# A decoder layer's up projections with seven block products for eight in half of the k groups, weight sums made by adding DMAs and VectorE, and the hidden columns in three parts

## The chip, the cores and the metric

The kernel runs on one core of a Trainium2 chip, as one launch. The metric is the device time of a launch in microseconds; the median of three runs of the kernel before is 2240.55 us.

## The reference, cut to what matters

One decoder layer on 256 tokens of 2048 features: a SwiGLU network, a token-mixing block, and a second SwiGLU network, each followed by a LayerNorm over the sum with its input. All is float32. The change lies in the two SwiGLU networks:

```
def swiglu(x, w_up, w_down):                    # x [256, 2048], D_FF = 5632
    a, u = jnp.split(x @ w_up, 2, axis=-1)      # w_up [2048, 2 * 5632]
    return (jax.nn.silu(a) * u) @ w_down        # w_down [5632, 2048]

h = layer_norm(ALPHA * h + 0.5 * swiglu(h, w_ffn1_up, w_ffn1_down), ln1_g, ln1_b)
...
h = layer_norm(ALPHA * h + 0.5 * swiglu(h, w_ffn2_up, w_ffn2_down), ln3_g, ln3_b)
```

## The kernel before, in words

**Split products.** Every large matrix product is made from float32r parts. A float32 page is split into h, its rounded value, and l, the rest, so that h + l is the page exactly (`split`, L90 to L93): ScalarE (ACT) writes h (L92), then VectorE (DVE) writes l = page - h (L93). A product of two split matrices takes three matmuls on TensorE (PE): ah with wh, ah with wl, al with wh (L133). One matmul has 128 rows of k, 128 tokens (stationary) and 512 weight columns (moving), and adds into a PSUM bank of 128 x 512.

**A gemm** (L121) makes 512 output columns for both token tiles (tt = 0, 1). It goes over groups of 512 rows of k. For each group the weights, 1 MB, come in one DMA on the queue of SyncE (SP) into one of three `raw` buffers (L104 to L106), are split as two halves of 128 x 1024 into `wh` and `wl` (four buffers of each), and each half feeds 2 kt x 2 tt x 3 = 12 matmuls. A half can be split only when one of the four `wh` and `wl` pairs is free again, that is, when PE is through with the half four before it.

**A SwiGLU network** (`ffn`, L188). The hidden width has 11 columns of 512 (j). A column takes two gemms of four groups, a with the weights up[j] and u with up[11 + j]: 2 x 4 x 24 = 192 matmuls. Then ACT makes tanh of a (L206), DVE makes silu(a) * u from the two accumulators (L207, L208), and `place` turns the result back to features by 8 transposes on PE (L166) and a split into two pages (L92, L93); `later` and `tick` put that behind the first group of the next column's products. After all 11 columns the down product runs: four gemms of 11 groups (`project_norm`, L215), whose accumulators DVE adds to the residual (L235).

**Order of the work.** A scheduler orders the instructions on each engine when the program is built, and every engine then runs its own list strictly in that order, waiting on semaphores. DMAs are issued on three queues: SP (weights), ACT (the input x transposed, `in_xT`, L185) and POOL (GpSimd's software queue: residuals L223, scales L228, rows of results L267). `project_norm` issues the residuals' loads after the last column.

**The start.** x is loaded from `in_xT` page by page on ACT's queue (L185) beside the first weights, each page split before the products of its group.

Of the kernel before, what the change touches and what calls it, by code (L numbers as in the profile page):

```python
# [9 lines left out]
F32 = mybir.dt.float32  # L10
# [26 lines left out]
GL0 = 10  # L37


class Layer:  # L40
# [32 lines left out]
    def page(self, dt=F32, tag="pg"):  # L73
        return self.tile(tag, [P, 1024], dt, 27 if tag == "pg" else 6)
# [4 lines left out]
    def tmp(self, shape=(P, 512), dt=F32):  # L79
        return self.tile("tmp", list(shape), dt, 4)  # L80

    def acc(self):
        self.n += 1
        return self.ps.tile([P, 512], F32, name=f"acc_{self.n}", tag="acc", bufs=4)

    def tr(self):
        self.n += 1
        return self.ps.tile([P, 512], F32, name=f"tr_{self.n}", tag="tr", bufs=4)
# [10 lines left out]
    def raw(self, shape=(P, 4, 512)):  # L99
        return self.tile("raw", list(shape), F32, 3)  # L100

    def load_w(self, src, paged=False, cut=None):
        """[128, 4, 512] of weights -> two halves of (h, l); cut(i) goes with half i."""
        raw = self.raw()  # L104
        if cut is None:
            self.nc.sync.dma_start(raw, src)  # L106
        out = []
        for i in range(2):
            if cut is not None:
                cut(i)  # L110
                self.nc.sync.dma_start(raw[:, 2 * i:2 * i + 2, :], src[:, 2 * i:2 * i + 2, :])
            if paged:
                h, l = (self.page(F32R).rearrange("p (k n) -> p k n", k=2) for _ in range(2))
            else:
                h = self.tile("wh", [P, 2, 512], F32R, 4)
                l = self.tile("wl", [P, 2, 512], F32R, 4)
            self.split(h, l, raw[:, 2 * i:2 * i + 2, :])
            out.append((h, l))
# [35 lines left out]

    def act_pages(self, hp, lp):
        """Pages of four k tiles by 256 tokens -> act() of gemm."""
# [5 lines left out]
    def transpose4(self, src):  # L162
        """[128, 512] -> four [128, 128] transposes side by side in PSUM."""
# [9 lines left out]
    def to_feature(self, src, hpage, lpage, tt, scale=None):  # L173
        """[128 tokens, 512] in SBUF -> h and l of the four k tiles in the pages."""
# [7 lines left out]
    def load_split_T(self, src, hp, lp, i, c=slice(0, 1024), paged=False):  # L182
        """Columns c of page i of src [128, 16, 256]."""
# [4 lines left out]
    def ffn(self, xh, xl, w_up, w_down, resid, g, b, finish, before_last=None, before=None, cut=None,  # L188
# [3 lines left out]
        hh, hl = [], []  # L192

        def place(ts, ph, pl):
            for tt in range(2):
                self.to_feature(ts[tt], ph, pl, tt)
            yield

        for j in range(NFF):
            a = self.gemm(act, w_up[j], 4, head=4 if j == 0 and before is None else 0, before=before if j == 0 else None,  # L200
                          cut=cut if j == 0 else None)
            u = self.gemm(act, w_up[NFF + j], 4)
            ph, pl = self.page(F32R), self.page(F32R)
            ts = [self.tmp(), self.tmp()]
            for tt, t in enumerate(ts):
                nc.scalar.activation(t, a[tt], AF.Tanh, scale=0.5)  # L206
                nc.vector.scalar_tensor_tensor(t, t, 1.0, a[tt], op0=ALU.add, op1=ALU.mult)  # L207
                nc.vector.scalar_tensor_tensor(t, t, 0.25, u[tt], op0=ALU.mult, op1=ALU.mult)  # L208
            self.later(place(ts, ph, pl))
            hh.append(ph)  # L210
            hl.append(pl)
        self.project_norm(self.act_pages(hh, hl), w_down, KF // 4, resid, g, b, finish, before_last,
                          4 if before_last is None else 2, filler)

    def project_norm(self, act, w, groups, resid, g, b, finish, before_last=None, tail=4, filler=None):  # L215
        """finish(LN(ALPHA * resid + act @ w))."""
        nc = self.nc
        z = [self.page(tag="gt") for _ in range(ND)]
        gb = [self.page(tag="gt" if i < 2 else "pg") for i in range(ND)]
        stats = [self.tile("stats", [P, ND, 6], F32, 2) for _ in range(2)]  # L220
        for n in range(ND):
            for tt in range(2):
                self.mark = nc.gpsimd.dma_start(z[n][:, 512 * tt:512 * tt + 512],  # L223
                                                resid[tt * P:(tt + 1) * P, 512 * n:512 * n + 512])
        with self.after_mark():
            for n in range(ND):
                for i, v in enumerate((g, b)):
                    nc.gpsimd.dma_start(gb[n][:, 512 * i:512 * i + 512],  # L228
# [461 lines left out]
```

## Time and profile before

| | |
|---|---|
| three runs | 2240.1, 2240.55, 2241.12 us; median 2240.55 |
| the profiled execution | span 2238.4 us from its first to its last instruction; no other time of its own is given, so what lies around the span is taken from the median: 2.15 us |
| PE busy | 2215.9 us, 99% of the span, 10056 matmuls |
| DVE busy | 1248.9 us, 56% |
| ACT busy | 958.2 us, 43% |
| DMA | 442 MB at a mean of 198 GB/s |

The share of busy time says who works, not who is waited for; the chain that ended last says that: 96% of it is PE. A busy PE is not PE at its fastest, since matmuls are pipelined (one shows some 390 ns while the next starts after some 227); the pace is read from stretches of the chain.

### The profile page before, as it was taken

Reading aid. Unit: us, or ns where it says so; the run is one execution under the profiler, and the core shown is the slowest. Engines: PE = TensorE matmul, PEld = TensorE weight load, DVE = VectorE, ACT = ScalarE, POOL = GpSimd, SP = SyncE. Lnnn points to the kernel's source line nnn. Section 1 sums busy time; section 2 is a strip of 40 time slices with the busy share of each in tenths; the row PEclk is TensorE's granted clock in tenths of the full one; section 3 lists DMA queues with packets and bytes.
Section 4 is the critical chain, followed back from the end, with each engine's and each line's share of the span. In section 5 each row is a group of like instructions: output and inputs, shape, how many; then the busy total and the mean of one; then the engine's idle time right before and its main releaser. Section 6 shows DMA issues by size and latency. Waiting matters only on the chain.

```text
span 2238.4 us, 24924 instructions
## 1 busy us (share of the span) xinstructions
PE 2215.9 (99%) x10056; PEld 1838.5 (82%) x10056; DVE 1248.9 (56%) x1404; ACT 958.2 (43%) x1075; POOL 51.2 (2%) x93
## 2 busy tenths in 40 slices
PE   8999999999999999999999999999999999999997
PEld 6888888888888888888888888878888888888886
DVE  5555555554455757675566556675555555454445
ACT  4444444443334444554444444444444444443332
POOL 0000000010000100000000000010000000000000
PEclk9999999999999999999999999999999999999999
DMA  7555555565556645455655556666555555565553
GB/s 261 191 188 188 188 188 188 189 253 205 199 188 228 233 170 182 169 184 188 207 179 194 199 193 220 235 221 239 188 188 188 189 190 191 188 211 197 188 192 128
DMA packets 65956, 442.34 MB, mean 198 GB/s; under 512 B 7905, under 2 KB 7905, under 8 KB 15537
## 3 DMA queue, kind: packets, MB, share of 16 engines
q1 hardware_dynamic: 57888, 414.21, 52.4%
q0 software_dynamic: 6656, 22.36, 3.4%
q10 hardware_dynamic: 1296, 4.19, 0.5%
q8 instruction: 78, 1.28, 0.2%
q14 instruction: 38, 0.30, 0.0%
HBM read 434.44 MB, written 6.29 MB: 197 GB/s over the span
## 4 chain that ended last, share of the span: by engine, by line
PE 96%; DVE 2%; DMA 1%; issue 0%; ACT 0%; POOL 0%; POOLq 0%; ACTq 0%; DVEq 0%
PE acc L133 93%; PE tr L166 2%; PE tr L282 1%; DMA pg<-in_xT 1%; DVE wl L93 0%; DVE pg L562 0%; DMA tmp<-in_w_pool 0%; DVE gt L252 0%; DVE m L561 0%; PE tr L314 0%; DVE pg L93 0%; DVE gt L254 0%; DVE stats L236 0%; DVE gt L235 0%; POOL mv L245 0%
## 5 line engine op out<-in xcount | busy, mean ns | idle before, releaser
L133 PE MATMUL acc<-wh,pg 128*128 128x512 f32 x5120 | 1594.2, 390 | 0.0
L93 DVE TENSOR_TENSOR wl<-raw,wh 128x1024 fp32r<-128x1024 f32 x772 | 944.4, 1224 | 917.2 <-ACT wh L92 916.7
L92 ACT CAST wh<-raw 128x1024 fp32r<-128x1024 f32 x772 | 812.7, 1054 | 1130.6 <-PE acc L133 1099.2
L133 PEld LDWEIGHTS acc<-wh,pg 128*128 128x128 f32 x5120 | 961.2, 188 | 198.3
L133 PE MATMUL acc<-wl,pg 128*128 128x512 f32 x2560 | 996.4, 389 | 0.0
L133 PEld LDWEIGHTS acc<-wl,pg 128*128 128x128 f32 x2560 | 480.7, 188 | 98.0
L133 PE MATMUL acc<-wh,gt 128*128 128x512 f32 x1056 | 332.8, 391 | 7.8 <-ACT wh L92 7.2
L133 PEld LDWEIGHTS acc<-wh,gt 128*128 128x128 f32 x1056 | 198.9, 189 | 49.3 <-ACT wh L92 7.2
L133 PE MATMUL acc<-wl,gt 128*128 128x512 f32 x528 | 206.4, 391 | 1.0 <-DVE wl L93 1.0
L133 PEld LDWEIGHTS acc<-wl,gt 128*128 128x128 f32 x528 | 99.6, 189 | 22.2 <-DVE wl L93 1.8
L92 ACT CAST pg<-tr 128x512 fp32r<-128x512 f32 x82 | 44.7, 586 | 20.4 <-PE tr L166 19.8
L93 DVE TENSOR_TENSOR pg<-tr,pg 128x512 fp32r<-128x512 f32 x82 | 52.5, 682 | 0.6 <-ACT pg L92 0.3
L206 ACT ACTIVATE tmp<-acc 128x512 f32<-128x512 f32 x44 | 26.2, 595 | 26.0 <-PE acc L133 26.0
L207 DVE SCALAR_TENSOR_TENSOR tmp<-tmp,acc 128x512 f32<-128x512 f32 x44 | 30.1, 684 | 10.3 <-ACT tmp L206 10.3
L133 PE MATMUL acc<-pg,pg 128*128 128x512 f32 x144 | 34.5, 392 | 0.8 <-DVE pg L93 0.7
L133 PEld LDWEIGHTS acc<-pg,pg 128*128 128x128 f32 x144 | 26.8, 188 | 7.1 <-DVE pg L93 1.6
L166 PEld LDWEIGHTS tr<-ident,tmp 128*128 128x128 f32 x240 | 27.9, 140 | 3.9
L166 PE MATMUL tr<-ident,tmp 128*128 128x128 f32 x240 | 31.0, 272 | 0.0
L208 DVE SCALAR_TENSOR_TENSOR tmp<-tmp,acc 128x512 f32<-128x512 f32 x44 | 28.1, 680 | 0.0
L235 DVE SCALAR_TENSOR_TENSOR gt<-gt,acc 128x512 f32<-128x512 f32 x24 | 15.7, 682 | 21.5 <-PE acc L133 21.5
L282 PE MATMUL tr<-pg,pg 128*128 128x256 f32 (+2 forms) x168 | 26.3, 302 | 0.0
L93 DVE TENSOR_TENSOR pg<-raw,pg 128x1024 fp32r<-128x1024 f32 x18 | 21.7, 1217 | 4.5 <-ACT pg L92 4.5
(99 smaller groups left out, 418.4 us busy)
## 6 DMA issues: line engine op xcount, KB each, us to landing
raw<-in_up SPq DMA_DIRECT2D x175, 1024.0 KB, 4.8
raw<-in_down SPq DMA_DIRECT2D x88, 1024.0 KB, 4.8
raw<-in_w_in SPq DMA_DIRECT2D x88, 1024.0 KB, 4.8
raw<-in_w_out SPq DMA_DIRECT2D x16, 1024.0 KB, 5.1
raw<-in_w_kv SPq DMA_DIRECT2D x8, 1024.0 KB, 5.0
raw<-in_br_att SPq DMA_DIRECT2D x8, 1024.0 KB, 4.8
h_d<-gt POOLq DMA_DIRECT2D x16, 256.0 KB, 3.6
raw<-in_br_pool SPq DMA_DIRECT2D x4, 1024.0 KB, 4.8
```

Of the source, the lines that this page charges most:

```text
L92: self.nc.scalar.copy(h, src)
L93: self.nc.vector.tensor_sub(l, src, h.bitcast(F32))
L133: nc.tensor.matmul(accs[tt], lhsT=a, rhs=b, start=kt == 0 and i == 0, stop=kt == kts - 1 and i == 2)
L166: self.nc.tensor.transpose(t[:, i * P:(i + 1) * P], src[:, i * P:(i + 1) * P], self.ident)
L206: nc.scalar.activation(t, a[tt], AF.Tanh, scale=0.5)
L207: nc.vector.scalar_tensor_tensor(t, t, 1.0, a[tt], op0=ALU.add, op1=ALU.mult)
L208: nc.vector.scalar_tensor_tensor(t, t, 0.25, u[tt], op0=ALU.mult, op1=ALU.mult)
L235: nc.vector.scalar_tensor_tensor(zz, zz, ALPHA, accs[tt], op0=ALU.mult, op1=ALU.add)
L282: self.nc.tensor.matmul(out, lhsT=a, rhs=b, start=start and i == 0, stop=stop and i == 2)
```

## The change

**Seven products for eight.** For each column but the first of a network, a and u are made together by `seven`. In a group of 512 rows of k the operands are seen as 2 x 2 blocks: tokens 0 to 127 and 128 to 255, k in two halves of 256, and the two weight matrices w0 = up[j], w1 = up[11 + j]. In groups 0 and 1 seven block products, in Winograd's form of Strassen's scheme, replace eight; groups 2 and 3 keep eight products, with one of the token operands replaced by a difference so that they can share the banks. A column so takes 2 x 7 x 6 + 2 x 48 = 180 matmuls for 192, in seven PSUM banks. Ten columns in each of the two networks are made so: 20 columns.

**Sums of tokens** are made once per network (`forms`) on DVE, beside the first column.

**Sums of weights.** In a seven group three halves are loaded and split as they are: b00, b10 (w0) and b11 (w1). Then b00 becomes b00 + b01 by a DMA on POOL's queue that adds from HBM (L230), is split (t1), becomes t1's sum plus b11 by DVE (L239), is split (t2), becomes that plus b10 by DVE (L243), and is split (t4); b11 becomes b11 + b01 by a second adding DMA (L241), which needs L239 to have read b11, and is split (t3). So a seven group has seven splits for four, two DVE sums and two adding DMAs of 512 KB.

**Combination.** Behind a column ACT copies bank 1 and DVE makes seven sums and differences of the banks (L283 to L289) before the SwiGLU arithmetic (now L351, L352).

**Columns in three parts.** `HIDDEN` cuts the 11 columns into 4, 4 and 3. After each part the down product runs over that part's groups alone, and its four results are added to the residual's pages (`Norm.add`). The residuals' loads (`Norm.load`) are called after the first part, the scales' before the last down product.

**Buffers.** `raw` is nine buffers of half the size (a weight group comes as two DMAs of 512 KB), pages are 23 and 6 for 27 and 6, tmp six for four, and the accumulators and transposes share all eight PSUM banks. x takes ordinary pages, not those of tag gt. Loads of the memory input stand at the first two groups of the last down gemm.

```diff
+PAGES = dict(pg=23, gt=6)
+HIDDEN = ((0, 4), (4, 8), (8, NFF))
+SEVEN = (True, True, False, False)
...
-        return self.ps.tile([P, 512], F32, name=f"acc_{self.n}", tag="acc", bufs=4)
+        return self.ps.tile([P, 512], F32, name=f"acc_{self.n}", tag="ps", bufs=8)
...
-    def raw(self, shape=(P, 4, 512)):
-        return self.tile("raw", list(shape), F32, 3)
+    def raw(self, shape=(P, 2, 512)):
+        return self.tile("raw", list(shape), F32, 9)
...
+    def forms(self, hp, lp, modes):
...
+            a = self.page()
+            nc.vector.tensor_add(a, hp[g].bitcast(F32), lp[g].bitcast(F32))
+            if seven:
+                q = a.rearrange("p (j k i t) -> p i j k t", j=2, k=2, i=2)
+                f = self.page()
+                fv = f.rearrange("p (f k t) -> p f k t", f=4, k=2)
+                nc.vector.tensor_sub(fv[:, 0], q[:, 1, 0], q[:, 1, 1])
+                nc.vector.tensor_sub(fv[:, 1], fv[:, 0], q[:, 0, 0])
+                nc.vector.tensor_sub(fv[:, 2], q[:, 0, 0], q[:, 1, 0])
+                nc.vector.tensor_add(fv[:, 3], q[:, 0, 1], fv[:, 1])
+                h, l = self.page(F32R), self.page(F32R)
+                self.split(h, l, f)
...
+        def singles(g, end):
+            b00, b10 = self.load_half(w0[g], 0), self.load_half(w0[g], 1)
+            b11 = self.load_half(w1[g], 1)
+            s00 = self.halves(b00)
+            nc.gpsimd.dma_start(b00, w1[g][:, 0:2, :], accum_op=ALU.add)
+            product(g, 1, quarter(g, 0, 0), s00, g == sevens[-1])
+            s10 = self.halves(b10)
+            product(g, 2, quarter(g, 0, 1), s10, end)
+            s11 = self.halves(b11)
+            product(g, 3, form(g, 3), s11, end)
+
+            def sums():
+                t1 = self.halves(b00)
+                nc.vector.tensor_add(b00, b00, b11)
+                product(g, 5, form(g, 0), t1, end)
+                nc.gpsimd.dma_start(b11, w1[g][:, 0:2, :], accum_op=ALU.add)
+                t2 = self.halves(b00)
+                nc.vector.tensor_add(b00, b00, b10)
+                product(g, 6, form(g, 1), t2, g == sevens[-1])
+                t3 = self.halves(b11)
+                product(g, 7, form(g, 2), t3, g == sevens[-1])
+                t4 = self.halves(b00)
+                product(g, 4, quarter(g, 1, 1), t4, end)
+
+            return sums
...
+        behind = None
+        for g in range(groups):
+            end = g == groups - 1
+            if modes[g]:
+                after = singles(g, end)
+            else:
+                eight(g, end)
+                after = None
+            if behind is not None:
+                behind()
+            behind = after
+            self.tick()
...
+        u, c00, v, c11 = (self.tmp() for _ in range(4))
+        nc.scalar.copy(u, banks[1])
+        nc.vector.tensor_add(c00, u, banks[2])
+        nc.vector.tensor_add(u, u, banks[6])
+        nc.vector.tensor_add(v, u, banks[7])
+        nc.vector.tensor_sub(u, banks[5], u)
+        nc.vector.tensor_sub(c11, banks[5], v)
+        nc.vector.tensor_add(u, u, banks[3])
+        nc.vector.tensor_add(v, v, banks[4])
+        return [[c00, u], [v, c11]]
...
+        for lo, hi in HIDDEN:
+            hh, hl = [], []
+            for j in range(lo, hi):
+                if j == 0:
+                    a = self.gemm(act, w_up[0], 4, head=4 if before is None else 0, before=before, cut=cut)
+                    forms = self.forms(xh, xl, SEVEN)
+                    u = self.gemm(act, w_up[NFF], 4)
+                else:
+                    c = self.seven(act, forms, SEVEN, w_up[j], w_up[NFF + j])
+                    a, u = ([c[tt][i] for tt in range(2)] for i in range(2))
...
+            if lo == 0:
+                norm.load()
+            if last:
+                norm.load_scales()
+            w = [w_down[n][lo:hi] for n in range(ND)]
+            norm.add(self.act_pages(hh, hl), w, hi - lo, lo == 0, last, before_last,
+                     3 if before_last is None else 2)
```

**How it moves instructions.** The first place is DVE's list where one column ends and the next begins. Before (wl is a half's l, L208 the last step of the SwiGLU arithmetic, pg<-tr the turned result):

```order
L93 TENSOR_TENSOR wl_991<-raw_988,wh_990 128x1024
L93 TENSOR_TENSOR wl_995<-raw_988,wh_994 128x1024
L93 TENSOR_TENSOR wl_1039<-raw_1036,wh_1038 128x1024
L208 SCALAR_TENSOR_TENSOR tmp_978<-tmp_978,acc_838 128x512
L208 SCALAR_TENSOR_TENSOR tmp_979<-tmp_979,acc_839 128x512
L93 TENSOR_TENSOR wl_1043<-raw_1036,wh_1042 128x1024
L93 TENSOR_TENSOR wl_1073<-raw_1070,wh_1072 128x1024
L93 TENSOR_TENSOR wl_1077<-raw_1070,wh_1076 128x1024
```

In the change the same place on DVE reads as follows; L286 is the first combination that needs the column's last product, and wl_1185, wl_1196 belong to group 1 of the next column, whose group 0 has been split before these rows:

```order
L286 TENSOR_TENSOR tmp_1109<-acc_873,tmp_1109 128x512
L287 TENSOR_TENSOR tmp_1112<-acc_873,tmp_1111 128x512
L288 TENSOR_TENSOR tmp_1109<-tmp_1109,acc_817 128x512
L289 TENSOR_TENSOR tmp_1111<-tmp_1111,acc_908 128x512
L351 SCALAR_TENSOR_TENSOR tmp_1123<-tmp_1123,tmp_1110 128x512
L96 TENSOR_TENSOR wl_1185<-raw_1178,wh_1184 128x1024
L352 SCALAR_TENSOR_TENSOR tmp_1123<-tmp_1123,tmp_1109 128x512
L351 SCALAR_TENSOR_TENSOR tmp_1124<-tmp_1124,tmp_1111 128x512
L96 TENSOR_TENSOR wl_1196<-raw_1180,wh_1195 128x1024
L352 SCALAR_TENSOR_TENSOR tmp_1124<-tmp_1124,tmp_1112 128x512
```

Eight combining steps and two splits stand there where two steps stood. The rows that follow directly on DVE, with the third split of group 1 and the sums of group 0 (raw_1131 is its b00, raw_1133 its b10, raw_1135 its b11):

```order
L96 TENSOR_TENSOR pg_1122<-tr_1171,pg_1121 128x4x128
L96 TENSOR_TENSOR wl_1206<-raw_1182,wh_1205 128x1024
L96 TENSOR_TENSOR wl_1216<-raw_1131,wh_1215 128x1024
L239 TENSOR_TENSOR raw_1131<-raw_1131,raw_1135 128x1024
L96 TENSOR_TENSOR wl_1229<-raw_1131,wh_1228 128x1024
L243 TENSOR_TENSOR raw_1131<-raw_1131,raw_1133 128x1024
L96 TENSOR_TENSOR wl_1241<-raw_1135,wh_1240 128x1024
L96 TENSOR_TENSOR wl_1252<-raw_1131,wh_1251 128x1024
```

They are t1, the first sum, t2, the second sum, t3 and t4 in that order, all behind the combining of the column before.

The second place is ACT's list at the program's start, with the loads of x (in_xT) that ACT issues. Before:

```order
L185 DMA pg_82<-in_xT 128x512
L185 DMA pg_91<-in_xT 128x512
L185 DMA pg_124<-in_xT 128x1024
L92 ACT_TABLE_LOAD
L92 CAST gt_71<-pg_82 128x512
L92 CAST wh_87<-raw_81 128x1024
```

In the change:

```order
L322 DMA pg_81<-in_xT 128x512
L95 ACT_TABLE_LOAD
L95 CAST pg_71<-pg_81 128x512
L95 CAST wh_87<-raw_85 128x1024
L322 DMA pg_91<-in_xT 128x512
L95 CAST wh_97<-raw_95 128x1024
L322 DMA pg_125<-in_xT 128x1024
L95 CAST pg_71<-pg_91 128x512
L95 CAST wh_131<-raw_129 128x1024
L95 CAST wh_137<-raw_135 128x1024
L95 CAST pg_72<-pg_125 128x1024
L95 CAST wh_171<-raw_169 128x1024
```

The second and third loads have moved behind casts of weights; the fourth, pg_165, follows wh_171, and the fifth, pg_205, follows the cast of the fourth.

The third place is POOL's queue at the start. Before, its first loads of x's rows (L223) follow the last up column. In the change they stand right behind the constants:

```order
L540 DMA pscale_67<-in_pool_scale 128x4
L476 DMA gt_1478<-in_x 128x512 x2
L476 DMA gt_1479<-in_x 128x512 x2
L476 DMA gt_1480<-in_x 128x512 x2
L476 DMA gt_1481<-in_x 128x512 x2
L485 DMA gt_5103<-in_g 128x512
L485 DMA gt_5103<-in_b 128x512
L485 DMA gt_5104<-in_g 128x512
L485 DMA gt_5104<-in_b 128x512
L230 DMA raw_437<-in_up 128x1024
```

Twelve loads of 256 KB, 3 MB, are so issued at the start, ahead of the first adding DMA.

## Rows read from the trace of the kernel before

**Rows 1.** The page, part 1: busy time, share and instructions of each engine.
```profile
PE 2215.9 (99%) x10056; PEld 1838.5 (82%) x10056; DVE 1248.9 (56%) x1404; ACT 958.2 (43%) x1075; POOL 51.2 (2%) x93
```
**Rows 2.** Waits, whole span: who waited for whom, us in total, times, longest.
```profile
ACT wh L92 <- PE acc L133: 1099.2, 680, 5.7
DVE wl L93 <- ACT wh L92: 916.7, 699, 3.2
...
PE acc L133 <- ACT wh L92: 7.2, 1, 7.2
```
**Rows 3.** Chain of work, 100 to 200 us: start, us, what.
```profile
105.88 43.54 PE acc L133 x192
149.42 0.88 PE tr L166 x8
150.29 43.54 PE acc L133 x192
```
**Rows 4.** Busy time in windows: one column; the down product. Columns: PE, PEld, DVE, ACT, POOL, clock, DMA, GB/s.
```profile
105.88:150.29 44.41, 44.41 (x201) 36.86 (x201) 23.28 (x22) 18.93 (x21) 0.00 (x0) 1.00 0.52 189
...
505.60:761.30 255.70, 255.70 (x1130) 211.67 (x1130) 140.54 (x142) 103.80 (x101) 8.00 (x11) 1.00 0.59 207
```
**Rows 5.** Groups by line: busy us, mean ns | idle before, releaser.
```profile
L93 DVE TENSOR_TENSOR wl<-raw,wh 128x1024 fp32r<-128x1024 f32 x772 | 944.4, 1224 | 917.2 <-ACT wh L92 916.7
L92 ACT CAST wh<-raw 128x1024 fp32r<-128x1024 f32 x772 | 812.7, 1054 | 1130.6 <-PE acc L133 1099.2 <-issue 7.5 <-ACT gt L549 6.6
```
**Rows 6.** Timeline of DVE, two dense stretches: start, us, engine, line, what.
```profile
758.42 1.41 DVE L254 SCALAR_TENSOR_TENSOR gt<-gt,mv,pg 128x512 f32<-128x512 f32 x2
759.75 2.35 DVE L93 TENSOR_TENSOR wl<-raw,wh 128x1024 fp32r<-128x1024 f32 x2
...
764.53 4.27 DVE L93 TENSOR_TENSOR pg<-tr,pg 128x512 fp32r<-128x512 f32 x7
...
1493.32 1.22 DVE L93 TENSOR_TENSOR pg<-raw,pg 128x1024 fp32r<-128x1024 f32 x1
1494.45 1.22 DVE L93 TENSOR_TENSOR wl<-raw,wh 128x1024 fp32r<-128x1024 f32 x1
```
**Rows 7.** DMA issues of POOL's queue in four windows: KB each, us to landing.
```profile
tmp<-in_b_gate POOLq DMA_DIRECT2D x1, 256.0 KB, 4.7
pg<-in_consts POOLq DMA_DIRECT2D x1, 512.0 KB, 5.5
raw<-in_band POOLq DMA_DIRECT2D x1, 1024.0 KB, 6.2
pg<-in_consts POOLq DMA_DIRECT2D x1, 512.0 KB, 9.4
```
**Rows 8.** Chain of work at the start: start, us, what.
```profile
1.66 10.94 DMA pg<-in_xT
...
12.64 7.64 DMA pg<-in_xT
...
22.67 37.92 PE acc L133 x166
```
**Rows 9.** Busy time in one window at the start; columns as in rows 4.
```profile
10.00:15.00 5.00, 5.00 (x18) 3.95 (x17) 2.72 (x4) 2.81 (x4) 0.00 (x0) 1.00 0.98 363
```
**Rows 10.** Timeline of PE at the start.
```profile
7.24 1.22 PE L133 MATMUL acc<-wh,gt 128*128 128x512 f32 x2 [7.24 <-ACT wh L92]
...
10.09 0.63 PE L133 MATMUL acc<-wh,gt 128*128 128x512 f32 x1
10.52 0.63 PE L133 MATMUL acc<-wl,gt 128*128 128x512 f32 x1
...
13.50 0.40 PE L133 MATMUL acc<-wl,gt 128*128 128x512 f32 x1
13.74 0.62 PE L133 MATMUL acc<-wh,gt 128*128 128x512 f32 x2
```

More of the change, by code (lines that the diff above doesn't have):

```diff
@@ L73, in page @@
     def page(self, dt=F32, tag="pg"):
-        return self.tile(tag, [P, 1024], dt, 27 if tag == "pg" else 6)
+        return self.tile(tag, [P, 1024], dt, PAGES[tag])
     def pages(self, n, dt=F32R, tags=()):
@@ L110, in load_w @@
                 cut(i)
[L111 to L118, printed above, removed]
+            out.append(self.halves(self.load_half(src, i), paged))
         return out
@@ L153, in gemm @@
         return accs
+    def forms(self, hp, lp, modes):
+        nc = self.nc
+        out = []
+        for g, seven in enumerate(modes):
+            a = self.page()
[11 more added lines that the diff above has]
+            else:
+                q = a.rearrange("p (k i t) -> p i k t", k=4, i=2)
+                f = self.tmp()
+                nc.vector.tensor_sub(f.rearrange("p (k t) -> p k t", k=4), q[:, 0], q[:, 1])
+                both = self.page(F32R)
+                h, l = both[:, :512], both[:, 512:]
+                self.split(h, l, f)
+            out.append((h, l))
+        return out
@@ new lines, in seven, with product, quarter, form @@
+    def seven(self, act, forms, modes, w0, w1):
+        nc = self.nc
+        banks = {}
+        groups = len(modes)
+        sevens = [g for g in range(groups) if modes[g]]
+        first = set()
+        def product(g, bank, lhs, w, last):
+            if bank not in banks:
+                banks[bank] = self.acc()
+            for k in range(2):
+                ah, al = lhs(k)
+                for i, (a, b) in enumerate(((ah, w[0]), (ah, w[1]), (al, w[0]))):
+                    nc.tensor.matmul(banks[bank], lhsT=a, rhs=b[:, k, :], start=bank not in first,
+                                     stop=last and k == 1 and i == 2)
+                    first.add(bank)
+        def quarter(g, i, j):
+            return lambda k: act(4 * g + 2 * j + k, i)
+        def form(g, i):
+            return lambda k: tuple(v[:, (2 * i + k) * P:(2 * i + k + 1) * P] for v in forms[g])
+        def singles(g, end):
[21 more added lines that the diff above has]
+            return sums
+        def eight(g, end):
+            b00, b10 = self.load_half(w0[g], 0), self.load_half(w0[g], 1)
+            b01, b11 = self.load_half(w1[g], 0), self.load_half(w1[g], 1)
+            s00 = self.halves(b00)
+            product(g, 2, quarter(g, 0, 0), s00, False)
+            product(g, 4, quarter(g, 1, 0), s00, False)
+            s10 = self.halves(b10)
+            product(g, 2, quarter(g, 0, 1), s10, end)
+            product(g, 4, quarter(g, 1, 1), s10, end)
+            s01 = self.halves(b01)
+            product(g, 3, form(g, 0), s01, False)
+            product(g, 5, quarter(g, 1, 0), s01, False)
+            s11 = self.halves(b11)
+            product(g, 3, form(g, 1), s11, end)
+            product(g, 5, quarter(g, 1, 1), s11, end)
+        behind = None
[3 more added lines that the diff above has]
+                after = singles(g, end)
+            else:
+                eight(g, end)
[4 more added lines that the diff above has]
+            self.tick()
+        assert behind is None
+        u, c00, v, c11 = (self.tmp() for _ in range(4))
[8 more added lines that the diff above has]
+        return [[c00, u], [v, c11]]
@@ L191, in ffn @@
         act = self.act_pages(xh, xl)
-        hh, hl = [], []
+        norm = Norm(self, resid, g, b)
+        forms = None
         def place(ts, ph, pl):
@@ L196, in place @@
                 self.to_feature(ts[tt], ph, pl, tt)
[L197 to L211, printed above, removed]
@@ L258, in norm_to_feature, with project_norm @@
+        norm.finish(finish, filler)
+    def project_norm(self, act, w, groups, resid, g, b, finish):
+        norm = Norm(self, resid, g, b)
+        norm.load()
+        norm.load_scales()
+        norm.add(act, w, groups, True, True, None, 4)
+        norm.finish(finish)
     def norm_to_feature(self, dram):
@@ L361, in layer_kernel @@
     h2_d = L.dram.tile([SEQ, D_MODEL], F32, name="h2_d")
-    xh = L.pages(ND, tags=("gt",) * 3)
-    xl = L.pages(ND, tags=("gt",) * 3)
+    xh = L.pages(ND)
+    xl = L.pages(ND)
     mem = ([], [])
     def load_mem(g):
-        if g in (4, 6, 8, 10):
+        for _ in range(2 if g < 2 else 0):
             for p in mem:
```

144 lines of the change are left out of this document (89 added, 55 removed).

## The prediction

> **What bounds the kernel now.** I read the page's busy times first: PE is busy for 99% of the span, DVE for 56%, ACT for 43% [rows 1]. Busy does not say bound, so the waits came next. ACT's casts wait for PE 1099.2 us in all, DVE's splits wait for ACT 916.7 us, and PE waits for either of them once, 7.2 us at the start [rows 2]: the weights' chain DMA, ACT, DVE always runs ahead until its four buffers are full. Third, the chain of work over two up columns: 192 matmuls in 43.54 us, then 8 transposes in 0.88, and again [rows 3]. So a column lasts 44.4 us, and a matmul 43.54 / 192 = 0.2268 us. In a column DVE works 23.3 us and ACT 18.9 [rows 4]. PE alone sets the time here, and only fewer matmuls or a new wait can change it.
>
> The median of the runs is 2240.55 us, the profiled span 2238.4. I make the sum on the span's pieces and add it to the median; the 2.15 us around the span stay.
>
> **What the change removes.** 12 matmuls in each of 20 columns: 12 x 0.2268 = 2.72 us a column, 54.4 us in all. PE's own work in a column becomes 180 x 0.2268 + 0.88 = 41.7 us.
>
> **What it adds on DVE.** Dense stretches give the pace: a 128 x 1024 step follows the last after 1.13 us, though one lasts 1.22; seven 512-wide steps with PSUM take 4.27, so 0.60 each; two 512-wide steps with both inputs in SBUF take 1.33 to the next start, 0.665 each [rows 6]. A column needs 22 splits and 4 sums (26 x 1.13 = 29.4), 7 combinations and 2 turned results (9 x 0.60 = 5.4) and 4 SwiGLU steps (2.7): 37.5 us. ACT needs 22 casts of 1.05 [rows 5] and some small ones, 26 us. Both are under 41.7, so by sums alone nothing is lost. But the order on DVE decides, and I follow one column with a column before it.
>
> **The path through a column.** Zero is the end of the last product before.
> - DVE has by then split the three single halves of the new group 0 (its four buffers allow no more), which keep PE for 18 x 0.2268 = 4.1 us. The rest of DVE's list stands behind L286, which needs that last product: four combinations (4 x 0.60 = 2.4), four SwiGLU steps (2.66), a turned result (0.6), three splits of group 1 and t1 (4 x 1.13 = 4.5), then the first sum, which has to wait until t1 is through and be through itself (1.3). It ends at 11.5 us.
> - Only then can POOL issue the second adding DMA; ACT's cast of t3 waits for it, and the casts of t4 and of group 2 stand behind that on ACT. From before I know plain loads on this queue: 256 KB land after 4.7 us, 512 KB after 5.5 and, beside much traffic, 9.4, 1 MB after 6.2 [rows 7]. An adding DMA of 512 KB reads 512 KB in HBM and 512 KB in SBUF, so I take the row of 1 MB, **6.2 us**, with 4.7 and 9.4 as the ends. It lands at 17.7.
> - Cast of t3 1.05, its split 1.22, split of t4 1.13, then five matmuls of t4's product and three transposes (1.46): PE starts group 2 at 22.6 us. Without waits it would have started at 4.1 + 4.1 + 5.4 + 0.9 = 14.5.
> - Group 2 and the sums of group 1: t1 of group 1 gets a buffer when the first half of group 2 is done (2.72); cast 1.05, split 1.22, sum 1.25, DMA 6.2, cast 1.05, splits 1.22 and 1.13, five matmuls 1.13: 17.0 us. PE's own work for this stretch is 72 x 0.2268 = 16.3, so this wait is nearly hidden.
> - Group 3: 48 x 0.2268 = 10.9.
>
> The sum is 22.6 + 17.0 + 10.9 = **50.5 us against 44.4, 6.1 more**. 14 of the 20 columns are so. The two behind a network's first column lack the combinations: 47.1, 2.7 more each. The four that follow a down product have neither: the first sum is through at 4.1 + 1.05 + 1.22 + 1.22 = 7.6, and the column takes 46.2, 1.8 more each. Together 14 x 6.1 + 2 x 2.7 + 4 x 1.8 = **98 us**. The first adding DMA (L230) needs no place in the sum: it is issued some 5 us before zero, and t1's turn on ACT comes past 4.
>
> With 4.7 us for the DMA the three kinds take 48.3, 44.9 and 44.0, in all 54 us more; with 9.4 every column is 6.4 longer than in the sum, in all 226 more. Even a DMA that cost nothing would leave 11.5 + a cast, t2, the second sum, t3 and t4 = 17.4, so 46.1 for a full column.
>
> The Trainium skill, DMA: Bandwidth & Descriptors (Anatomy of one DMA, SWDGE path), puts a DMA of this queue at about 2.0 us and its bytes at 436 GB/s, an estimate of 3.2 us for 512 KB, by which the sum would be some 25 us. The rows speak against it: 256 KB, 2.6 by that rule, took 4.7.
>
> **The start.** x's pages load on ACT's queue. Before, three loads went out at once, and the page that ended last landed after 10.94 + 7.64 us; PE runs without a stop from 22.67 [rows 8], while the DMA engines are busy all the time (0.98) [rows 9]. Now loads two to five stand behind casts on ACT, each cast waiting for weights or a buffer, and 3 MB of residuals and scales are issued on POOL's queue at the same time. Two loads of some 7.6 us are so put behind each other, of which the products of three k groups hide about half: I take **8 us**, between 2 (loads of 4.7 us) and 12.
>
> **At no cost.** The token sums (`forms`), at most 18 DVE steps or 14 us per network, lie beside a first column in which DVE idles some 21 us [rows 4]; without that cover they would cost 28 us in all. The 32 further additions of down results take 19 us of DVE beside down products, where DVE works 140.5 us of 255.7 [rows 4]. Five loads of half a megabyte for four per seven group are 20 MB more, where the DMA engines are busy for half the time (0.52) [rows 4]; their own waits are in the path above. The middle of the layer keeps its products; shared PSUM banks and smaller buffers may move it by 5 us either way.
>
> The sum: 2240.55 + 98 + 8 = **2347 us**.
>
> **Rivals.**
> - *The chain is hidden.* If DVE's 37.5 us and the DMAs stayed beside PE's 41.7, the saving would come through: 2240.55 - 54.4 + 8 = 2194. For it speak the busy sums, and the 1.5 us of idle time before each split now. Against it: L286 stands ahead of group 1's splits and t1. It decides at a column path of 44.4 us, and the path has 46.1 with a free DMA, so it needs DVE's steps to be a fifth shorter than their rows.
> - *The adding DMA lands in about 3 us.* Then the full column takes 46.9 and the total is 2274. No row of that queue is so short. This is also what the page's rule above gives.
> - *PE's clock falls in the gaps.* Between t2's and t3's products PE would idle some 3.7 us. At the start, after 7.24 us without work, matmuls come 0.43 us apart (10.09 to 10.52), as at 1.2 GHz, and later 0.24 (13.50 to 13.74) [rows 10]; the granted clock printed there is 1.00 [rows 9], so I go by the spacing. Some 11 matmuls ran so, 0.2 us longer each: 2.3 us a gap, 46 us in 20 columns, in all 2393. Against it: the gap is half as long. The Trainium skill, TensorE: Matmul & The Clock Gate (Part 1), says that the throttled state is the default and that activity lifts it; the start agrees, no row shows a gap of this length later.
> - *The adding DMA is slow*, 9.4 us: 2347 + 128 = 2475. For it speaks that no row shows an adding DMA.
>
> **How the numbers follow.** The forecast (DMA of 5 to 7.5 us, 2305 to 2400) has 0.56, the fallen clock 0.18, the slow DMA 0.13, the fast one 0.06, the hidden chain 0.07. The range runs from 2290, the 4.7 us end with a start of 2 us and some slack, to 2480, the slow DMA; it leaves out the two quick cases. No change, within 0.2% (which is what a measurement of this kernel can tell), lies in none of the cases but between them: 0.01. Faster is the hidden chain, 0.07; slower 0.92.
>
> **What would show it.** Right: a column of 50 us, PE waiting in it once for the cast or split of t3 for several us; L241 issues that land after 6 us; DVE busy for three quarters of the up stretch; the down products at 0.227 us a matmul as before; PE's continuous run starting some 8 us later. Wrong: columns under 44 us, no PE wait behind t3, or waits of PE that end on a PSUM bank instead; matmuls 0.43 us apart behind the gaps mean the third rival.

## The result and the profile after

The changed kernel takes **2428.88 us** (median of 4 runs, 2427.76 to 2433.55) against 2240.84 us for the kernel before beside it: ratio 1.0844, 95% interval 1.0831 to 1.0856. It is slower, as forecast, and inside the range, but by 188 us where the sum said 106. It lies outside the narrower band, 2305 to 2400 us, that the forecast gives for a DMA of 5 to 7.5 us. The profiled span is 2427.9 us, 189.5 longer than before's.

The page, part 1, and the waits of PE, which before waited once, 7.2 us [rows 1, 2]; columns of a wait: in total, times, longest.

```profile
PE 2258.0 (93%) x9816; PEld 1822.4 (75%) x9816; DVE 1600.8 (66%) x1812; ACT 1086.2 (45%) x1223; POOL 120.2 (5%) x174
```
```profile
PE acc L215 <- ACT wh L95: 91.3, 65, 3.9
PE acc L215 <- DVE wl L96: 40.9, 54, 0.9
PE tr L303 <- DVE gt L524: 9.9, 2, 9.5
```

PE does 240 matmuls fewer, and is busy 42 us longer: some of them run at half speed. Its waits are now in the new products (L215), 119 of them in 20 columns. Three columns in windows (before [rows 4]: 44.41 us, PE without a gap, DVE 23.28, ACT 18.93, clock 1.00, DMA 0.52), the first and last of these full ones, the middle one behind a down product:

```profile
114.00:167.99 53.99, 46.67 (x189) 35.93 (x188) 38.73 (x39) 24.95 (x27) 3.40 (x4) 0.91 0.65 176
308.69:358.65 49.96, 44.88 (x182) 35.58 (x180) 34.00 (x31) 23.05 (x23) 3.41 (x4) 0.93 0.67 188
2295.74:2349.80 54.06, 47.33 (x190) 36.15 (x188) 38.73 (x39) 24.92 (x27) 4.78 (x7) 0.91 0.67 198
```

DVE's 38.7 us are the prediction's 37.5; nothing is busy for 54 us. The chain of work through one column shows what is: start, us, what (left out: hand-overs, and more steps of the kinds shown).

```profile
168.19 0.69 DVE tmp L286
...
171.28 1.15 DVE wl L96
...
172.98 0.82 POOL raw L230
173.79 5.97 issue
179.77 6.21 DMA raw<-in_up
...
186.09 1.05 ACT wh L95
...
187.16 0.92 DVE wl L96
...
188.13 0.79 PE acc L215
...
192.50 12.30 PE acc L215 x54
...
204.82 1.06 ACT wh L95
```

It begins with the combination L286, which needs the last product of the column before. The "issue" of 5.97 us is POOL waiting for the first sum (L239); then come the adding DMA L241, 6.2 us to landing, and t3's cast and split. The timelines of POOL, DVE and ACT show the same:

```profile
179.77 0.85 POOL L241 DMA_DIRECT2D raw<-in_up  x1 [5.98 <-DVE raw L239]
```
```profile
175.88 2.35 DVE L96 TENSOR_TENSOR wl<-raw,wh 128x1024 fp32r<-128x1024 f32 x2
178.26 1.22 DVE L239 TENSOR_TENSOR raw<-raw,raw 128x1024 f32<-128x1024 f32 x1
...
187.16 4.63 DVE L96 TENSOR_TENSOR wl<-raw,wh 128x1024 fp32r<-128x1024 f32 x4 [4.09 <-ACT wh L95]
```
```profile
186.09 3.89 ACT L95 CAST wh<-raw 128x1024 fp32r<-128x1024 f32 x4 [5.53 <-DMA raw<-in_up]
```

PE's timeline behind that wait, and the same stretch in windows: matmuls 0.43 us apart at a granted clock of 0.57, which is the 1.2 GHz level for most of it; back at 1.00 from 191.

```profile
187.18 0.79 PE L215 MATMUL acc<-wh,pg 128*128 128x512 f32 x1 [3.88 <-ACT wh L95]
...
189.36 1.05 PE L215 MATMUL acc<-wh,pg 128*128 128x512 f32 x2
190.21 0.56 PE L215 MATMUL acc<-wl,pg 128*128 128x512 f32 x1
190.61 0.40 PE L215 MATMUL acc<-wh,pg 128*128 128x512 f32 x1
```
```profile
178.00:183.00 5.00, 3.35 (x14) 2.07 (x12) 3.82 (x4) 1.04 (x1) 0.85 (x1) 1.00 0.33 34
187.00:191.00 4.00, 3.66 (x9) 2.57 (x10) 3.84 (x4) 2.97 (x4) 0.00 (x0) 0.57 0.35 119
191.00:205.00 14.00, 14.00 (x65) 11.54 (x64) 8.74 (x8) 4.87 (x6) 0.85 (x1) 1.00 0.82 252
```

Where the 189.5 us went, from the starts of the first matmul of each stage:

| stage | before | after | difference |
|---|---|---|---|
| to the second column's first product | 54.98 | 63.69 | +8.7 |
| 20 columns and the down products, both networks | 1368.5 | 1537.7 | +169.2 |
| the middle and the second network's first column | 803.0 | 814.6 | +11.6 |

The down products alone keep their 0.227 us a matmul, without a gap. In the 20 columns, adding up the spacing of all matmul starts, PE stands idle for some 164 us and loses some 56 us to the slower clock; 54.4 are saved.

### The profile page after: what moved, and what is told of

Read it like the earlier page. It is cut to its first block, busy times and chain, and to the rows that moved or that the text cites. A ratio compares the mean times of both kernels' runs of the same rounds, so it can differ in the third digit from the quotient of the medians.

```text
span 2427.9 us, 26418 instructions
## 1 busy us (share of the span) xinstructions
PE 2258.0 (93%) x9816; PEld 1822.4 (75%) x9816; DVE 1600.8 (66%) x1812; ACT 1086.2 (45%) x1223; POOL 120.2 (5%) x174
## 4 chain that ended last, share of the span: by engine, by line
PE 65%; DMA 13%; issue 12%; DVE 7%; ACT 3%; POOL 1%; POOLq 0%; ACTq 0%; DVEq 0%; SPq 0%
PE acc L141 44%; PE acc L215 19%; DMA raw<-in_up 12%; DVE wl L96 4%; ACT wh L95 3%; PE tr L303 1%; PE tr L398 1%; DMA pg<-in_xT 1%; POOL raw L230 1%; DVE raw L239 0%; DVE tmp L286 0%; DVE tmp L351 0%; DVE tmp L289 0%; DVE tmp L287 0%; DVE tmp L288 0%
## 5 line engine op out<-in xcount | busy, mean ns | idle before, releaser
L96 DVE TENSOR_TENSOR wl<-raw,wh 128x1024 fp32r<-128x1024 f32 x894 | 1077.4, 1222 | 738.2 <-ACT wh L95 734.8
L95 ACT CAST wh<-raw 128x1024 fp32r<-128x1024 f32 x894 | 926.7, 1051 | 1199.7 <-PE acc L141 581.8
L141 PE MATMUL acc<-wh,pg 128*128 128x512 f32 x3632 | 1138.5, 392 | 12.4 <-ACT wh L95 7.5
L215 PE MATMUL acc<-wh,pg 128*128 128x512 f32 x2400 | 804.2, 410 | 91.3 <-ACT wh L95 91.3
L141 PEld LDWEIGHTS acc<-wh,pg 128*128 128x128 f32 x3632 | 684.1, 189 | 155.9 <-ACT wh L95 7.5
L141 PE MATMUL acc<-wl,pg 128*128 128x512 f32 x1816 | 709.0, 390 | 0.6 <-DVE wl L96 0.6
L215 PEld LDWEIGHTS acc<-wh,pg 128*128 128x128 f32 x2400 | 470.6, 196 | 217.1 <-ACT wh L95 124.1
L215 PE MATMUL acc<-wl,pg 128*128 128x512 f32 x1200 | 494.9, 412 | 41.7 <-DVE wl L96 40.9
L141 PEld LDWEIGHTS acc<-wl,pg 128*128 128x128 f32 x1816 | 342.4, 189 | 71.1 <-DVE wl L96 1.3
L215 PEld LDWEIGHTS acc<-wl,pg 128*128 128x128 f32 x1200 | 236.2, 197 | 117.9 <-DVE wl L96 67.1
L230 POOL DMA_DIRECT2D raw<-in_up x40 | 34.2, 855 | 882.7 <-DMA raw<-in_up 485.5
L241 POOL DMA_DIRECT2D raw<-in_up x40 | 34.1, 853 | 489.8 <-DVE raw L239 273.6
L243 DVE TENSOR_TENSOR raw<-raw,raw 128x1024 f32<-128x1024 f32 x40 | 49.0, 1225 | 1.4
L239 DVE TENSOR_TENSOR raw<-raw,raw 128x1024 f32<-128x1024 f32 x40 | 49.0, 1224 | 1.3
L303 PE MATMUL tr<-ident,tmp 128*128 128x128 f32 x240 | 40.3, 285 | 0.0
L351 DVE SCALAR_TENSOR_TENSOR tmp<-tmp,tmp 128x512 f32<-128x512 f32 x40 | 27.3, 682 | 0.0
L352 DVE SCALAR_TENSOR_TENSOR tmp<-tmp,tmp 128x512 f32<-128x512 f32 x40 | 27.2, 681 | 0.0
```

What stands on the lines that cost most here:

```text
L141: nc.tensor.matmul(accs[tt], lhsT=a, rhs=b, start=kt == 0 and i == 0, stop=kt == kts - 1 and i == 2)
L215: nc.tensor.matmul(banks[bank], lhsT=a, rhs=b[:, k, :], start=bank not in first, stop=last and k == 1 and i == 2)
L230: nc.gpsimd.dma_start(b00, w1[g][:, 0:2, :], accum_op=ALU.add)
L239: nc.vector.tensor_add(b00, b00, b11)
L241: nc.gpsimd.dma_start(b11, w1[g][:, 0:2, :], accum_op=ALU.add)
L243: nc.vector.tensor_add(b00, b00, b10)
```

## The experiments

All times are medians, ratios against the kernel before on the same chip. **Theory A** is the prediction's: the column's sums stand in a chain (combinations, splits, first sum, adding DMA, cast, split) for which PE waits; start and middle cost apart from it. Its rivals: the parts, halves and shared banks cost the time; VectorE's load does; the adding DMAs alone do; the clock does.

**e1, the parts alone.**
```diff
-                    forms = self.forms(xh, xl, SEVEN)
...
-                    c = self.seven(act, forms, SEVEN, w_up[j], w_up[NFF + j])
-                    a, u = ([c[tt][i] for tt in range(2)] for i in range(2))
+                    a = self.gemm(act, w_up[j], 4)
+                    u = self.gemm(act, w_up[NFF + j], 4)
```


> All eight products in every column (two plain products of four k groups, as before the change), no token sums, no adding DMAs; the three parts of the hidden layer, the half-size loads, the shared PSUM banks and the new loads of x stay. Theory A (the column's loss comes from the sums' chain): columns of 44.4 us again, PE without gaps in them; what is left is the start (+8.7 us in the changed kernel's trace) and the middle with the second network's first column (+11.6), so about 2261 us, and 2249 if the middle's 11.6 belong to the sums too. Theory B (the loss comes from halves, shared banks and fewer pages): columns stay above 48 us, over 2330 us.

Measured 2262.55 us, 1.0097 [1.0082, 1.0112]. One column:
```profile
108.39:152.87 44.48, 44.48 (x202) 36.82 (x201) 23.29 (x23) 18.93 (x20) 0.00 (x0) 1.00 0.61 189
```
The columns are before's again, so 166 of the 188 us belong to the seven products. The other 22 are nearly all the start (8.7) and the middle (11.6), whose one long wait this kernel has too:
```profile
PE tr L303 <- DVE gt L523: 9.9, 2, 9.4
```

**e8, the banks apart.** Tags of the PSUM tiles: "acc" 4 and "tr" 4 for "ps" 8.

> e1 (all eight products) with the PSUM banks parted as before the change: four for products, four for transposes, and not one set of eight. Everything else as e1. Theory A (the wait of 9.6 us at the end of the middle comes from the order in which the shared banks made the scheduler put the second token tile's transposes: ahead of the second network's first products, and not behind them): that wait goes, 2262.5 - 9.6 = 2253 us; the start's 8.7 us stay. Rival (it comes from fewer pages or from the half-size loads): 2262 as e1.

Measured 2249.96 us, 1.0041 [1.0026, 1.0055]: 12.6 less than e1, 9.6 expected, and that wait is gone:
```profile
PE tr L303 <- DVE gt L523: 0.8, 2, 0.5
```
So the shared banks moved the order: in e1 PE has the second token tile's transposes ahead of the next network's first products, and stands still until LayerNorm has made their data. What the other 3 us are is not shown. The prediction's "5 us either way" for the middle was too narrow.

**e2, the gap filled.**
```diff
+                for _ in range(2 if g == sevens[0] else 0):
+                    product(g, 6, form(g, 1), t2, True)
+                    first.discard(6)
                 product(g, 6, form(g, 1), t2, g == sevens[-1])
```


> The changed kernel with the product of t2 in the first seven-product group done three times (twice for nothing, each time starting the bank anew; the result is the same): 12 more matmuls in each of 20 columns, 240 in all, 54 us of PE work at 0.227 us each, put into the idle time of 3 to 4 us ahead of t3. Theory A with the clock as its second term (idle time lowers PE's clock, 2.8 us a column): nothing else waits for these products, the idle time before t3 shrinks to about 1.3 us, matmuls behind it stay at 0.227 us, and the kernel gets faster by up to 55 us, to about 2375. Rival (the slow matmuls come from memory ports or from the adding DMA's traffic, not from idle time): they stay at 0.43 us, the time stays at 2429. Rival (PE work is on the path): 2429 + 54 = 2483.

Measured 2427.82 us (2419.16 to 2432.38), 1.0843 [1.0823, 1.0862]: no change. The mean granted clock rose from 0.965 to 0.987, and the loss to slow matmuls in the columns fell from 56 to 30 us; 240 more matmuls cost nothing; yet the median is only 1 us lower, with runs 13 us apart. The profile is that of the fastest run, 2419.16 us. The table compares it with the others (means over the 14 full columns, us from the column's first product to the first matmul of each step):

| | t1 | t3 | group 2 | its sums | group 3 | length |
|---|---|---|---|---|---|---|
| prediction | | 18.8 | 22.6 | | 39.6 | 50.5 |
| the change | 10.18 | 18.84 | 24.85 | 35.85 | 42.96 | 53.86 |
| e2 | 10.18 | 18.97 | 23.19 | 34.18 | 42.31 | 53.22 |
| e3 | 10.93 | 15.56 | 20.24 | 31.12 | 36.56 | 47.44 |
| e4 | 11.84 | 16.35 | 20.93 | 31.81 | 37.25 | 48.13 |

With the clock kept there, PE reaches group 2 1.7 us earlier, and then takes 1.0 us longer from the second group's sums to group 3. About 0.6 of that is the second group's adding DMA, which landed after 6.35 us in the mean where the change has 5.78; 3.4 loads of weights were in flight beside it for 2.1. The rest is t3's and t4's products, 4.4 us for 4.0. So PE meets the same chain again, with a longer DMA in it. The other 0.6 us a column is in this profile and hardly in the median, and half of the slow matmuls stayed: what the kernel would take with the clock kept everywhere is not shown.

**e3, the second adding DMA early.**
```diff
-            b11 = self.load_half(w1[g], 1)
+            b11, c11 = self.load_half(w1[g], 1), self.load_half(w1[g], 1)
...
+            nc.gpsimd.dma_start(c11, w1[g][:, 0:2, :], accum_op=ALU.add)
...
-                nc.gpsimd.dma_start(b11, w1[g][:, 0:2, :], accum_op=ALU.add)
...
-                t3 = self.halves(b11)
+                t3 = self.halves(c11)
```


> The second adding DMA gets a half of its own (the fourth quarter of the weights is loaded twice, 20 MB more from HBM in all) and so is issued at once and not behind VectorE's first sum. VectorE's steps and PE's order stay. Theory A: the 4 us wait before t3 and the 1 us wait in group 2 go; what is left per full column is VectorE's order, by the prediction's path 46.1 us, with about 1 us for the clock 47, against 53.9 now: 20 columns x 6 = 120 us less, about 2310. Rival (VectorE's load or the casts on ACT decide, the DMA only comes last): t3 waits as long for the steps in front of it, columns above 51 us, over 2370. Rival (traffic: more DMA makes every load late): as now or slower.

Measured 2308.01 us, 1.0298 [1.0283, 1.0314]; as expected. Ten of the 14 full columns last 46.80 us (the prediction's path without the DMA: 46.1), the other four 47.8 to 49.7. The second adding DMA's place in the chain cost 121 of the 188 us, the slow matmuls behind its wait included (mean granted clock 0.993).

**e4, all sums on VectorE.**
```diff
-            b11 = self.load_half(w1[g], 1)
+            b01, b11 = self.load_half(w1[g], 0), self.load_half(w1[g], 1)
...
-            nc.gpsimd.dma_start(b00, w1[g][:, 0:2, :], accum_op=ALU.add)
+            nc.vector.tensor_add(b00, b00, b01)
...
-                nc.gpsimd.dma_start(b11, w1[g][:, 0:2, :], accum_op=ALU.add)
+                nc.vector.tensor_add(b11, b11, b01)
```


> No adding DMA at all: the half that was added from HBM is loaded plainly and VectorE makes all four sums. VectorE has 4 more steps of 1.13 us a column, 42 us in all for PE's 41.7. Theory A (what counts is VectorE's order and the DMA's 6.2 us in the chain): two steps more on the chain of group 0 (2.3 us) for 6.2 us less; a full column of 46.1 + 2.3 = 48.4 us and about 2 for the clock, 50.5 against 53.9: about 2360. Theory C (VectorE's total load decides): column near 54, no gain or slower than 2429. Theory D (the adding DMAs alone are at fault): columns of 42 to 44 us, under 2260.

Measured 2315.78 us, 1.0338 [1.0323, 1.0354]: better than expected, because a fallen clock, put at 2 us a column, cost nothing. Two full columns:
```profile
109.00:157.12 48.12, 44.54 (x189) 35.48 (x188) 43.26 (x43) 25.46 (x27) 0.00 (x0) 0.96 0.53 175
613.56:661.69 48.13, 43.24 (x189) 34.29 (x188) 43.28 (x43) 25.57 (x27) 0.00 (x0) 1.00 0.52 175
```
In the first the clock fell (0.96) and PE was busy 1.3 us longer; the length is the same. PE waits here behind a chain of other engines, and the slower matmuls only fill its idle time. The path said 48.4.

**e5 and e6, the order of the groups.** Both: `SEVEN = (False, True, True, False)`; e6 with e3's early adding DMA.

> The groups in another order: eight products first, then the two seven-product groups, then eight (the sums of the second seven group end the column); the adding DMAs as in the change. Now a column begins with 10.9 us of products whose halves are split before its first instant, and VectorE's combinations and SwiGLU (5.7 us) lie beside them. Theory A: the waits of about 1 us before t1 and t2 go (3 us a column), but the second adding DMA still stands behind the first sum: that sum ends at about 18.4 us (t1's buffer comes free at 15), the DMA lands at 24.6, t3 is split at 26.9 where PE wants it at 21.8; one wait of 5 us in a column, the second seven group has a group of eight as cover. Column 41.7 + 5 = 47 us and up to 2 for the clock, 48.5: about 2325. Rival (the combinations don't matter, only the DMA chain does, twice): 52 us and more, 2390. Rival (hidden altogether): 42 us, 2205.

> The same order of groups, and the second adding DMA on a half of its own, issued early as in e3. Theory A: both causes are gone; VectorE's 37.5 us of steps lie beside PE's 41.7 in an order that PE need not wait for: columns of 41.7 to 43 us, no fallen clock in them, 20 x (1.4 to 2.7) less than before and the start and the middle as in e1 (2262): 2208 to 2235, faster than before. Rival (loads: nine halves of buffers hold eight for the two seven groups, so the last group's loads come late): a wait of 3 to 5 us a column, 45 to 47 us, 2270 to 2310. Rival (VectorE at 90% cannot be hidden): as e3, 2308.

Measured e5 2431.48 us, 1.0853 [1.0837, 1.087]; e6 2318.98 us, 1.0356 [1.0338, 1.0373]. Both expectations failed. In e5 (mean granted clock 0.966, in the change 0.965) t1 and t2 hardly wait, but t3 comes 25.7 to 30.4 us into the column (26.9 expected), and the second group's sums, for which a whole group of eight was to be the cover, wait again: t1 of that group gets its buffer only when the first half of group 3 is done, and from there the chain is longer than the products left. In e6 the chain of work has the *first* adding DMA in it, 8 us long, and ahead of that a split that frees a half buffer and the load into it:
```profile
110.26 1.15 DVE wl L96
...
111.42 8.68 DMA raw<-in_up
...
121.29 8.04 DMA raw<-in_up
...
129.43 1.05 ACT wh L95
```
On POOL's queue it stood behind the early one, which waited for its load, and that for one of nine half buffers, of which the two seven groups hold eight. This is the rival named there, by 9 us dearer. The first adding DMA's landings in e6: min, median, max 5.4, 8.4, 9.5 us, mostly with three adding DMAs in flight, where the change's L241 has
```profile
DMA to landing us min/median/max: 5.2/6.0/7.8
```

**e7, one seven group.** e3's early adding DMA and `SEVEN = (False, True, False, False)`.

> Seven products in one of the four groups only (the second), early adding DMA as in e3. 6 matmuls (1.36 us) less than before per column; VectorE has a seven group's 7 splits and 2 sums and three eight groups' 12 splits, 29 us of PE's 43. Theory A: columns of 43.1 us, 20 x 1.36 = 27 less than e1's 2262: 2235. Rival (each seven group costs a wait of its own of 1 to 2 us whatever its place): columns of 44.5 to 45, 2265 to 2275.

Measured 2235.73 us, 0.9978 [0.9968, 0.9987], as expected: 26.8 us less than e1, which has the same parts and eight products. One column, PE without a gap:
```profile
107.62:150.73 43.11, 43.11 (x195) 35.69 (x194) 33.34 (x34) 22.43 (x24) 1.70 (x2) 1.00 0.74 220
```
Never were two adding DMAs in flight here, and still the early one, with about five loads of weights beside it, took 7.7, 8.6, 9.3 us to land (min, median, max); the other, with about one, 5.3, 5.9, 6.5.

**e9, e7 with start and middle mended.** All x loads issued first on ACT's queue; the residual's loads on POOL's queue behind the third seven-product column's adding DMA; the second tile's transposes written into the next network's first product:
```diff
+            for tt, part in order:
+                while tt == 1 and self.hold:
+                    sink, *rest = self.hold.pop(0)
+                    sink(*rest)
```


> e7 (seven products in one group, early adding DMA) with the start and the middle mended: all five loads of x go out at the very beginning, the residual's loads on GpSimd's queue behind the adding DMAs of the first columns, and the second token tile's transposes at the end of the middle are written behind the next network's first products of the first tile. Theory A: the start gives back up to 8.7 us, the middle 9.6: 2235.7 - 8 - 9.6 = 2218 us, 1% under the kernel before. Rival (the start is bound by the bandwidth for x and the weights together, whatever the order of issue): 2226. Rival (both waits come back at another place): 2235.

Measured **2217.57 us**, 0.9897 [0.9883, 0.9912]: the fastest version, 1.0% under before, by the numbers expected. The wait in the middle went with the order alone, the banks still shared. The second column begins at 56.2 us (e7: 64.5), the middle is 10.1 us shorter. Which of the two edits at the start did it, x's loads or the residual's, was not tried apart.

**e10 and e11, seven groups alternating.** e3's early adding DMA and (True, False, True, False); (False, True, False, True).

> Seven products in groups 1 and 3, eight in groups 2 and 4, early adding DMAs, so that each seven group's sums lie beside a group of eight (in e6 two seven groups held eight of the nine half buffers at once and the adding DMA waited for its load). Theory A: the combinations at the column's start cost one wait of about 2.7 us behind the first three products, nothing waits after it: 41.7 + 2.7 = 44.4 us, up to 0.5 for the clock; the columns behind a down product 41: about 2255. Rival (two seven groups are too much for VectorE in any order): as e3, 2308.

> The same with the eight groups first: eight, seven, eight, seven; the sums of the last seven group end the column. Theory A: the combinations lie beside a group of eight (no 2.7 us), the second group's sums beside one too; the last group's singles and sums stand behind each other, where VectorE needs 10.2 us for PE's 9.5 and has run ahead by four halves: columns of 42 to 43 us, 2262 - 20 x (1.5 to 2.5) = 2212 to 2232. Rival (VectorE is behind at the end of a column, and the next column's combinations add to it): 46 to 48 us, 2300 to 2330.

Measured e10 2234.96 us, 0.9979 [0.997, 0.9988], 20 better than expected; e11 2458.97 us, 1.0972 [1.0956, 1.0988], the slowest of all and far above both of its expectations. e10 has the change's two seven groups and the same VectorE work, 38 us, and loses 1.6 us in most full columns:
```profile
106.56:150.14 43.58, 42.16 (x189) 34.43 (x188) 38.02 (x40) 24.98 (x27) 3.41 (x4) 1.00 0.82 240
```
```profile
110.42 0.85 PE L218 MATMUL acc<-wh,pg 128*128 128x512 f32 x3
112.69 0.50 PE L218 MATMUL acc<-wl,pg 128*128 128x512 f32 x1 [1.42 <-DVE wl L96]
```
That wait is for the split behind the combinations, as expected at another size (2.7); columns without combinations have none (41.75 and 40.80). In e11 a seven group's singles and sums stand next to each other at the column's end, so the first adding DMA, issued when the first single is split, is on the path too:
```profile
149.00 0.85 POOL L233 DMA_DIRECT2D raw<-in_up  x1 [7.11 <-DVE wl L96]
```
```profile
156.62 1.04 ACT L95 CAST wh<-raw 128x1024 fp32r<-128x1024 f32 x1 [4.25 <-DMA raw<-in_up]
```

**e12, e10 with e9's edits**, and a column that begins with two halves of its first eight group.

> e10's seven-product groups 1 and 3 with e9's start and middle, and one thing more: a column begins with the first two halves of its first eight group (5.4 us of products from two halves that are split before the column begins), then the first seven group's singles, then the eight group's other two halves, so that VectorE's 5.7 us of combinations and SwiGLU lie beside 9.5 us of products. Theory A: e10's wait of 1.6 us per column goes, columns of 41.75 us (40.8 behind a down product) as e10's columns without combinations have them; 20 columns 831 us against e9's 858, so 2217.6 - 27 = 2190 us. Rival (PSUM: the eight group's second bank has to wait for a combination, as in e11, 2.4 us): 2230. Rival (VectorE is behind and the wait moves): 2215.

Measured 2226.26 us, 0.9934 [0.9921, 0.9948]: the second rival, at 11 us more than its number. The wait at the combinations went, and came back as waits of 0.3 to 1.1 us further in, for ACT's casts (10.5 us in all) and VectorE's splits (8.2); full columns last 44.4 us in the mean, e10's 43.7:
```profile
96.47:140.79 44.32, 42.92 (x189) 34.34 (x188) 37.76 (x40) 24.89 (x27) 3.40 (x4) 1.00 0.82 235
54.72:96.47 41.75, 41.75 (x189) 34.57 (x188) 32.90 (x31) 24.34 (x25) 3.40 (x4) 1.00 0.76 211
```
The second row, a column without combinations, has no gap, with 33 us of work on VectorE; with the combinations, 38 us, PE waits, in this order as in e10's. e10 with e9's edits alone was not run. One group of seven (33 us with its combinations, e7) leaves PE without a gap.

## Why the prediction was right, and where it was short

**Right: what binds.** PE's 180 matmuls are not the limit, the chain is: e1 gives the columns back, e3 takes 121 us by moving one DMA, e10 wins with the same arithmetic, e7 and e9 with half of it, where the chain has cover. "The chain is hidden" was rightly rejected for this order, and is what e7 and, but for 1.6 us, e10 do.

**Right: the adding DMA, 6.2 us.** L241 lands after 6.0 us in the median (5.2 to 7.8); the first sum ends 11.5 us into the column, as the path said, and t3's products start at 18.84 us where it said 18.75 (landing 17.7, cast 1.05). The Trainium skill, DMA: Bandwidth & Descriptors (Anatomy of one DMA), leads to an estimate of 3.2 us for it; the trace speaks against that for an adding DMA: none of the 80 landed in less than 5.2 us. The size was in part luck. 6.0 lies between the rows of plain 512 KB (5.5) and 1 MB (6.2) [rows 7], and that adding costs what a second 512 KB would, the reason for taking the latter, no run tests.

**Short: the column, 53.9 for 50.5 us.** The path to group 2 was put at 22.6 us and took 24.85. t3 came on time; from its first matmul to group 2 the prediction had 3.85 us, the change took 6.0 and e2, with the clock kept, 4.22. This is the step that failed: matmuls behind the gap were counted at 0.227 us, and ran 0.43 apart. From group 2 to group 3 the working had 17.0 us; it took 18.1, of which about half a microsecond is POOL's issue behind the sum (L241 starts 0.53 us after L239's end there, 0.29 in the first group), which had no place in the path, and about as much the pace of t3 and t4, whose second matmul waits for a split. Columns behind a network's first one took 50.3 and 51.4 (47.1 predicted), those behind a down product 48.8 to 49.95 (46.2). Together 169 us with the down products, for 98. So the path was the right one and the range held, but the time left the band that goes with the DMA that was measured: the range's upper part was there for a slow DMA, and that the missing 82 us fell into it is luck.

**The rival of the fallen clock: its condition came true; what it cost is shown only in part.** The records show 1.2 GHz behind the gap in every column, after gaps of 2.7 to 4.1 us, shorter than the one at the start from which the rival was priced. It was a rival at 0.18 and should have been a term. Its price, 2.3 us a gap, is near the 1.8 us by which the step from t3 to group 2 is longer than in e2 (6.0 for 4.22). But its 46 us cannot simply be added: e2 took away half of the slow matmuls and its median is 1 us lower, and e4's columns have one length with and without them. The Trainium skill, TensorE: Matmul & The Clock Gate (Part 1), says that activity lifts the clock; the trace agrees, 0.57 from 187 to 191 us and 1.00 behind that.

**The start**, 8 us: 8.7 measured. ACT's casts of x waited 14.5 us there for its loads, four times; whether the order of issue or the 3 MB beside them made the loads late is not shown. **The middle**, within 5 us: 11.6, most of it the wait that the shared banks brought (e8). **At no cost**: the down products with their 32 further additions and the added traffic kept 0.227 us a matmul; the token sums stand beside a first column that lasts 56.1 us, and 56.6 in e1, which has none.

## What to carry to other kernels

Trading matmuls for sums is decided by where the sums stand: lay each chain (step that frees a buffer, sum, DMA, cast, split) beside products that last longer than it, start a transfer that reads and adds as soon as its target is loaded, and leave the engine that makes the sums some time free: VectorE with 33 us in a column of 43 held PE up nowhere (e7), with 38 in 43.6 it did by 1.6 us (e10). Here one group of seven with an early adding DMA won 1.0%, start and middle mended (e9); two groups with the DMA behind a sum lost 8.4%. And price a slower clock by what waits behind it, not by the matmuls that ran slow (e4).

## What was not expected of the hardware

- An adding DMA of 512 KB took 6.0 us in the median in the change, 8.4 with others of its kind in flight (e6), and 8.6 beside loads of weights with none of its kind in flight (e7); its issue held POOL 0.85 us.
- PE's clock fell in columns whose longest wait was some 2.6 us (e4), and not in e10's with 1.6 us (2.3 in one); of e4's 14 full columns, all with that same wait, eight had it and six had not.
- Which PSUM tiles share a set of banks changed the order of PE's instructions, and with it a wait of 9.4 us; parting the banks was worth 12.6 us (e1 to e8).
